# Experts of 144 to 192 slots: one gate-and-up product per pair of blocks, with the weights stationary, and empty slots left out of gathers and scatter-adds

## The chip, the cores and the metric

The kernel runs on one core of a Trainium2 chip. The metric is the device time of one execution in microseconds (us). The profile is one execution taken by the hardware profiler. Engines are named as there: PE is TensorE's matmul, PEld its weight load, DVE VectorE, ACT ScalarE, POOL GpSimd, SP SyncE, which issues the plain DMAs. A matmul's shapes are given as "stationary, moved": `128*128 128x512` holds 128 contracted rows by 128 columns in the array and moves 512 columns through it.

## What is computed

One block of a hybrid language model on 1024 tokens of width 1024: a mixer (two recurrent branches and an output projection), a layer norm, a mixture of experts, a layer norm. The change touches only the experts, which the reference computes like this:

```python
scores = sigmoid(h @ w_router)                 # 64 experts, 8 chosen for each token
for each expert e, on the tokens x that chose it, with their weights w:
    a = x @ w_gate[e]                          # 1024 -> 256
    u = x @ w_up[e]
    y = (silu(a) * u) @ w_down[e] * w          # 256 -> 1024
    acc[tokens] += y
out = layer_norm(alpha * h + acc + shared_expert(h))
```

## The kernel before

Everything is fp32. For precision each operand is split into a high part in a reduced fp32 format (`float32r`) and a low part, the remainder; a product is three matmuls, high x high, high x low and low x high (`mm3`, L135 to L137). The split of a weight piece of 128x1024 is a copy on ScalarE (L1529) and a subtraction on VectorE (L1530).

**Slots.** After the router, tokens are sorted on the chip into lists, one for each expert in the order of their counts. Each place in this order has a fixed cap (`CAPS`): 240, 208, three of 192, six of 176, nine of 160, eleven of 144, and 33 of 128, 112 or 96 slots. A place with more than 128 slots has two blocks, the first of 128 slots (m = 0), the second of the rest (m = 1). There are 64 + 31 = 95 blocks. Slots that no token fills point at rows behind the last token (index 1024 and up) of the gathered array `h1` and of the sum `acc`, which is 256 rows longer than the tokens for this purpose. Places with two blocks and places with one alternate in the order of work (`seq`), nearly throughout.

**A block's steps** (class `Block`): `fetch` gathers its rows of `h1` into an `xg` tile by an indirect DMA from GpSimd's queue, four blocks ahead; `turn_x` transposes them, 8 transposes of 128 columns into two PSUM tiles "tr" (there are two such banks), each of which ScalarE copies out as the high part (L173) and VectorE as the low part (L174); `gate_up` multiplies, with x stationary and the weights moved 512 columns at a time (256 of gate, 256 of up); `act` applies silu and the token's weight; `turn_a` transposes the result (L1431) and splits it; `down` multiplies by the down weights; `put` adds the rows to `acc` by an indirect DMA. A block of at most 64 slots is "packed": the high and low parts of x lie side by side as one stationary operand, so that two matmuls for each k do instead of three (`mm_packed`, L142 to L145), and the two halves of the result are added afterwards.

**The loop.** Iteration t works on block t and finishes block t-1. The instructions of PE, POOL and SP run in exactly the order of the code (`manual_schedule`); those of ScalarE and VectorE are ordered by a scheduler at build time. For PE an iteration is: the transposes of x of block t+1; half of gate and up of block t (k = 0 to 3); the matmuls that make a token list, if one is due (L1513); the transposes of the activation of block t-1; the other half of gate and up of t; down of t-1.

**Weights.** An expert's weights are six pieces of 128x1024, four of gate and up (two k each) and two of down. Raw pieces are loaded by SP ahead of time into nine tiles. The split halves live in eleven places that are used in turn, so a piece takes the place of the one eleven before it: piece 3 of an expert that of down piece 4 of the expert two before, and is split when that one's last reader is done. `splits` sends out splits at some 3 to 4.6 pieces an iteration, and always so many that the next block's gate and up have their four.

Of the kernel before, what the change touches and what calls it, by code (L numbers as in the profile page):

```python
# [19 lines left out]
P = 128  # L20
# [51 lines left out]
def block_kernel(tc, A, out):  # L72
# [1298 lines left out]
    between = mq.tile([P, 1], F32, name="between")  # L1371

    class Block:


        turn = 0

        def __init__(self, n, idx, wc, before=None):
            self.n, self.idx, self.wc, self.before = n, idx, wc, before

        def fetch(self):
            n = self.n
            self.x = mx.tile([P, D], F32, name="xg", tag="xg", bufs=XG)[:n]
            nc.gpsimd.indirect_dma_start(out=self.x, out_offset=None, in_=h1[:, :],  # L1384
                                         in_offset=bass.IndirectOffsetOnAxis(ap=self.idx, axis=0))

        def turn_x(self):

            n = self.n
            self.packed = n <= 64  # L1390
            if self.packed:
                xx = mt.tile([P, KT, P], F32R, name="xh", tag="xh", bufs=2)
                if n < 64:
                    nc.gpsimd.memset(xx[:, :, n:64].bitcast(F32), 0.0)
                self.xx, self.xh, self.xl = xx, xx[:, :, :n], xx[:, :, 64:64 + n]
            else:
                self.xh = mt.tile([P, KT, P], F32R, name="xh", tag="xh", bufs=2)[:, :, :n]
                self.xl = mt.tile([P, KT, P], F32R, name="xl", tag="xl", bufs=2)[:, :, :n]
# [16 lines left out]

        def act(self):
            n, pg = self.n, self.pg
            if self.packed:
                t = mo.tile([64, 512], F32, name="pk", tag="pk", bufs=2)[:n]
                nc.scalar.activation(t, pg[64:64 + n], AF.Copy)  # L1420
                nc.vector.tensor_add(t, pg[:n], t)
                pg = t
            self.a = ac = mo.tile([P, 256], F32, name="ac", tag="ac", bufs=2)[:n]
# [3 lines left out]
        def turn_a(self):  # L1427
            n = self.n
            pt = psum.tile([P, 4, P], F32, name="mm", tag="mm", bufs=3)
            for f in range(2):  # L1430
                nc.tensor.transpose(pt[:, f, :n], self.a[:, f * P:(f + 1) * P], ident[:n, :n])  # L1431
            if self.packed:
# [6 lines left out]
            nc.scalar.activation(self.ah, pt[:, 0:2, :n], AF.Copy)  # L1439
            nc.vector.tensor_sub(self.al, pt[:, 0:2, :n], self.ah.bitcast(F32))  # L1440

        def down(self):
# [3 lines left out]
            for half in range(2):  # L1446
# [3 lines left out]
                for f in range(2):  # L1450
# [3 lines left out]
                    else:  # L1454
                        mm3(py[:n], self.ah[:, f], self.al[:, f], wh, wl, f == 0, f == 1)
                if self.packed:
                    nc.scalar.activation(yh, py[64:64 + n], AF.Copy)
                    nc.vector.tensor_add(yh, py[:n], yh)
                else:
                    nc.scalar.activation(yh, py[:n], AF.Copy)  # L1460

        def put(self, apart=True):
            self.out = nc.gpsimd.indirect_dma_start(out=acc[:, :],  # L1463
                                                    out_offset=bass.IndirectOffsetOnAxis(ap=self.idx, axis=0),
                                                    in_=self.y, in_offset=None, compute_op=OP.add)
            if self.before is not None and apart:
                tc.declare_no_dep(self.out.ins, self.before.out.ins, reason="other tokens of the same expert")

    def finish_lists(pl, n, m, which=0):
# [8 lines left out]
        nc.vector.tensor_add(wc[:, :, 0], wc[:, :, 0], ls[:, :, 5])  # L1478
        return idx, wc

# [22 lines left out]
    def list_sums(q):  # L1503
# [12 lines left out]
        for m in range(nb):  # L1516
            n = min(P, cap - m * P)
            idx, wc = finish_lists(pl[:n, m], n, LG, m)
            for j in range(LG):
                x = seq[1 + q - LG + j]  # L1520
                nq = min(n, CAPS[x] - m * P)
                if nq > 0:
                    blocks[x, m] = Block(nq, idx[:nq, j], wc[:nq, j], before=blocks[x, 0] if m else None)

# [38 lines left out]
    with man:  # L1563
# [10 lines left out]
        for t in range(N + 1):  # L1574
# [43 lines left out]
    with tc.tile_pool(name="ov", bufs=1) as ov:  # L1618
# [41 lines left out]
        nc.vector.tensor_copy(tabr, pt[:, 0:2])  # L1660
        eidb = ov.tile([1, P], I32, name="eidb")
        nc.vector.tensor_copy(eidb, pt[0:1, 2])
# [3 lines left out]
        with tc.For_i(0, n_blocks, 1) as b:  # L1666
# [22 lines left out]
            for i in range(NT):  # L1689
                nc.tensor.matmul(pl[:, 0], oh[:, i], ab[:, i], start=i == 0, stop=i == NT - 1)  # L1690
            idx, wc = finish_lists(pl, P, 1)
            blk = Block(P, idx[:, 0], wc[:, 0])
            blk.fetch()
            blk.turn_x()
# [188 lines left out]
```

## Time and profile before

| | us |
|---|---|
| median of 3 runs | 2366.02 |
| lowest, highest | 2357.46, 2366.94 |
| the profiled execution, its own time | 2359.28 |
| its span, first to last instruction | 2357.4 |
| PE busy in the span | 2270.2 |
| DVE, ACT, POOL busy | 1570.2, 1102.0, 392.0 |
| bytes moved by DMA | 477.01 MB |

The span lies 1.9 us below the execution's own time. Busy is time with at least one instruction in flight; matmuls are pipelined, so a busy PE is not a PE at its peak, and the distance between the starts of two matmuls is the price of one rather than its duration. The experts take the stretch from about 1447 to 2312 us.

### The profile page before, as it was taken

How to read it: one execution, taken by the hardware profiler on the slowest of the kernel's cores; microseconds unless marked ns; L12 is line 12 of the kernel's file. 1: busy time of each engine (PE TensorE's matmuls, PEld its weight loads, DVE VectorE, ACT ScalarE, POOL GpSimd, SP SyncE). 2: the span in 40 equal slices, each digit the busy share in tenths (PEclk: the TensorE clock that was granted, in tenths of full speed). 3: DMA queues.
4: the chain of work that ended last, by engine and by line, in shares of the span. 5: the costliest groups of instructions: out<-in, count | busy, mean ns of one | idle time of the engine just before them, and what ended most of it. 6: DMA issues, size and time to landing. Idle time of an engine off the chain costs nothing.

```text
span 2357.4 us, 40161 instructions
## 1 busy us (share of the span) xinstructions
PE 2270.2 (96%) x15177; PEld 1804.1 (77%) x15177; DVE 1570.2 (67%) x3041; ACT 1102.0 (47%) x1853; POOL 392.0 (17%) x286
## 2 busy tenths in 40 slices
PE   7999999999999999999999999999999999999992
PEld 5797779877879977787887877777777777777761
DVE  6523886288614656214586677888888888888884
ACT  3432223223213265222332324677677777777773
POOL 4200000000000000000000001243434444433331
PEclk9999999999999999999999999999999999999996
DMA  7233244234322354536463336999999999999986
GB/s 289 89 115 123 74 139 131 91 114 130 106 81 82 121 180 170 165 99 232 146 225 115 119 124 221 301 336 319 327 324 336 321 314 319 327 307 324 305 285 166
DMA packets 203507, 477.01 MB, mean 202 GB/s; under 512 B 18720, under 2 KB 67552, under 8 KB 203312
## 3 DMA queue, kind: packets, MB, share of 16 engines
q1 hardware_dynamic: 180752, 396.13, 48.1%
q0 software_dynamic: 21520, 75.51, 13.4%
q8 instruction: 120, 1.97, 0.3%
q10 hardware_dynamic: 1040, 2.79, 0.3%
q14 instruction: 75, 0.61, 0.1%
HBM read 372.16 MB, written 103.78 MB: 202 GB/s over the span
## 4 chain that ended last, share of the span: by engine, by line
PE 85%; DVE 7%; DMA 3%; ACT 2%; issue 2%; POOL 0%; SPq 0%; DVEq 0%; POOLq 0%; ACTq 0%
PE mm L135 20%; PE mm L136 19%; PE mm L137 19%; PE sc L137 3%; PE tr L171 3%; PE sc L136 3%; PE sc L135 3%; PE mm L143 2%; PE mm L145 2%; PE sc L753 1%; PE po L1513 1%; DMA a<-qT 1%; PE sc L143 1%; PE mm L1431 1%; DVE wl L197 1%
## 5 line engine op out<-in xcount | busy, mean ns | idle before, releaser
L197 DVE TENSOR_TENSOR wl<-wraw,wh 128x1024 fp32r<-128x1024 f32 x118 | 141.4, 1221 | 205.4 <-ACT wh L196 201.3
L136 PE MATMUL mm<-hL,wh 128*128 128x512 f32 (+2 forms) x768 | 278.2, 362 | 0.0
L137 PE MATMUL mm<-hH,wl 128*128 128x512 f32 (+2 forms) x768 | 277.6, 361 | 0.0
L135 PE MATMUL mm<-hH,wh 128*128 128x512 f32 (+2 forms) x768 | 277.2, 361 | 0.0
L1463 POOL DMA_INDIRECT acc<-yo,idx x95 | 184.4, 1941 | 514.8 <-ACT xh L173 124.6
L135 PE MATMUL mm<-wh,hH 128*128 128x512 f32 x512 | 208.6, 407 | 2.6 <-ACT hH L349 1.8
L136 PE MATMUL mm<-wl,hH 128*128 128x512 f32 x512 | 209.0, 408 | 1.3 <-DVE wl L287 1.3
L137 PE MATMUL mm<-wh,hL 128*128 128x512 f32 x512 | 206.3, 403 | 0.0
L135 PEld LDWEIGHTS mm<-hH,wh 128*128 128x128 f32 x768 | 144.4, 188 | 17.2 <-issue 0.8
L136 PEld LDWEIGHTS mm<-hL,wh 128*128 128x128 f32 x768 | 144.4, 188 | 16.3 <-issue 0.5
L137 PEld LDWEIGHTS mm<-hH,wl 128*128 128x128 f32 x768 | 144.6, 188 | 15.6 <-issue 0.2
L196 ACT ACTIVATE wh<-wraw 128x1024 fp32r<-128x1024 f32 x118 | 122.7, 1056 | 54.0 <-PE mm L136 36.8
L1530 DVE TENSOR_TENSOR wl<-eraw,wh 128x1024 fp32r<-128x1024 f32 x112 | 135.4, 1216 | 14.9 <-ACT wh L1529 14.7
L1384 POOL DMA_INDIRECT xg<-h,idx x95 | 136.9, 1441 | 48.1 <-issue 22.8
L1530 DVE TENSOR_TENSOR wl<-wraw,wh 128x1024 fp32r<-128x1024 f32 x96 | 115.8, 1216 | 29.0 <-ACT wh L1529 28.6
L1529 ACT ACTIVATE wh<-eraw 128x1024 fp32r<-128x1024 f32 x112 | 117.2, 1061 | 19.0 <-PE mm L137 13.8
L135 PE MATMUL mm<-wh,xh 128*128 128x512 f32 (+3 forms) x296 | 123.7, 418 | 0.0
L135 PEld LDWEIGHTS mm<-wh,hH 128*128 128x128 f32 x512 | 98.2, 192 | 25.3 <-ACT hH L349 2.4
L136 PE MATMUL mm<-wl,xh 128*128 128x512 f32 (+3 forms) x296 | 117.1, 396 | 0.0
L137 PE MATMUL mm<-wh,xl 128*128 128x512 f32 (+3 forms) x296 | 116.9, 395 | 0.0
L137 PEld LDWEIGHTS mm<-wh,hL 128*128 128x128 f32 x512 | 97.7, 191 | 22.9 <-DVE hL L350 0.8
L136 PEld LDWEIGHTS mm<-wl,hH 128*128 128x128 f32 x512 | 98.0, 191 | 21.6 <-DVE wl L287 1.6
(550 smaller groups left out, 5424.9 us busy)
## 6 DMA issues: line engine op xcount, KB each, us to landing
eraw<-in_wexp_dram SPq DMA_DIRECT2D x210, 512.0 KB, 7.9
wraw<-in_wexp_dram SPq DMA_DIRECT2D x168, 512.0 KB, 6.9
wraw<-in_w_in_dram SPq DMA_DIRECT2D x72, 512.0 KB, 4.6
sgT<-st SPq DMA_DIRECT2D x32, 256.0 KB, 3.3
sg<-sgT SPq DMA_DIRECT2D x32, 256.0 KB, 4.2
wraw<-in_w_branch_a_dram SPq DMA_DIRECT2D x16, 512.0 KB, 5.0
wraw<-in_w_branch_b_dram SPq DMA_DIRECT2D x16, 512.0 KB, 6.9
wraw<-in_w_out_dram SPq DMA_DIRECT2D x16, 512.0 KB, 5.2
```

Of the source, the lines that this page charges most:

```text
L135: nc.tensor.matmul(o, ah, bh, start=start, stop=False)
L136: nc.tensor.matmul(o, ah, bl, start=False, stop=False)
L137: nc.tensor.matmul(o, al, bh, start=False, stop=stop)
L143: nc.tensor.matmul(o[:n], a[:, :n], bl, start=False, stop=False)
L145: nc.tensor.matmul(o[:w + n], a[:, :w + n], bh, start=False, stop=stop)
L171: nc.tensor.transpose(pt[:, k, :n], src[:, c:c + P], ident[:n, :n])
L196: nc.scalar.activation(h, raw, AF.Copy)
L197: (nc.gpsimd if j in on_pool else nc.vector).tensor_sub(l, raw, h.bitcast(F32))
L1384: nc.gpsimd.indirect_dma_start(out=self.x, out_offset=None, in_=h1[:, :], in_offset=bass.IndirectOffsetOnAxis(ap=self.idx, axis=0))
L1463: self.out = nc.gpsimd.indirect_dma_start(out=acc[:, :], out_offset=bass.IndirectOffsetOnAxis(ap=self.idx, axis=0), in_=self.y, in_offset= ...
L1529: nc.scalar.activation(h, raw, AF.Copy)
L1530: (nc.gpsimd if j in POOL_SPLITS else nc.vector).tensor_sub(l, raw, h.bitcast(F32))
```

## The change

For the 29 places of 144 to 192 slots the two blocks become a joined pair. The first block (`second` set) carries the matmuls of gate and up for both: `turn_x` transposes the x of both into one tile of up to 192 columns, and `gate_up` takes the weights as the stationary operand, in four column groups of 128 (two of gate, two of up), and moves the 144 to 192 columns of x through, for all eight k in each group. Its result comes out transposed, in two PSUM tiles, so that `turn_a` is not needed; `act` makes the activation for both blocks at once, and the tokens' weights are applied when `down`'s result is copied out. In the iteration of the second block (`joined`) `turn_x`, `gate_up`, `act` and `turn_a` do nothing. `down` and `put` of both blocks come together, in the iteration after it. `down` itself is unchanged (mm3 for the first block, packed for the second).

Slots without a token: both indirect DMAs get a bound of the last token, above which an index is skipped. As the rows skipped in a gather would otherwise be undefined, the five `xg` tiles become fixed ones that are cleared once. Places of 240 and 208 slots and those of one block work as before.

```diff
+    xgs = [mx.tile([P, D], F32, name="xg", tag="xg", bufs=XG) for _ in range(XG)]
+    for t in xgs:
+        nc.gpsimd.memset(t, 0.0)
...
+            self.joined = before is not None and n <= 64
+            if self.joined:
+                before.second = self
...
             nc.gpsimd.indirect_dma_start(out=self.x, out_offset=None, in_=h1[:, :],
-                                         in_offset=bass.IndirectOffsetOnAxis(ap=self.idx, axis=0))
+                                         in_offset=bass.IndirectOffsetOnAxis(ap=self.idx, axis=0),
+                                         bounds_check=T - 1, oob_is_err=False)
...
         def turn_x(self):
...
+            if self.joined:
+                return
+            if self.second is not None:
+                w = n + self.second.n
+                self.xh, self.xl = (mt.tile([P, KT, 192], F32R, name=q, tag=q, bufs=2)[:, :, :w] for q in ("xh", "xl"))
+                for b, c in ((self, slice(0, n)), (self.second, slice(n, w))):
+                    transpose_split(self.xh[:, :, c], self.xl[:, :, c], b.x, b.n)
+                return
...
         def gate_up(self, w, ks):
...
+            if self.second is not None:
+                n += self.second.n
+                if 0 in ks:
+                    self.w = w
+                    self.pg, self.pu = (psum.tile([P, 512], F32, name="mm", tag="mm", bufs=3)[:, :2 * n]
+                                        .rearrange("p (f n) -> p f n", f=2) for _ in range(2))
+                hs, ls = self.w()
+
+                for f in (0, 1) if 0 in ks else (2, 3):
+                    for k in range(KT):
+                        c = slice((k % 2) * 512 + f * P, (k % 2) * 512 + f * P + P)
+                        mm3((self.pg, self.pu)[f // 2][:, f % 2], hs[k // 2][:, c], ls[k // 2][:, c],
+                            self.xh[:, k], self.xl[:, k], k == 0, k == KT - 1)
+                return
...
         def act(self):
+            if self.joined:
+                return
             n, pg = self.n, self.pg
+            if self.second is not None:
+                w = n + self.second.n
+                a = mo.tile([P, 384], F32, name="ac", tag="ac", bufs=2)[:, :2 * w].rearrange("p (f n) -> p f n", f=2)
+                nc.scalar.activation(a, pg, AF.Silu)
+                nc.vector.tensor_mul(a, self.pu, a)
+                self.halves_a(a[:, :, :n])
+                self.second.halves_a(a[:, :, n:w])
+                return
...
         def turn_a(self):
+            if self.joined or self.second is not None:
+                return
...
         def down(self):
...
-                if self.packed:
+                if self.joined:
+                    nc.scalar.activation(yh, py[64:64 + n], AF.Copy, scale=self.wcp)
+                    nc.vector.scalar_tensor_tensor(yh, py[:n], self.wc, yh, op0=OP.mult, op1=OP.add)
+                elif self.packed:
...
+                elif self.second is not None:
+                    nc.scalar.activation(yh, py[:n], AF.Copy, scale=self.wc)
...
         def put(self, apart=True):
...
-                                                    in_=self.y, in_offset=None, compute_op=OP.add)
+                                                    in_=self.y, in_offset=None, compute_op=OP.add,
+                                                    bounds_check=T - 1, oob_is_err=False)
...
-            if prev:
-                prev.down()
+
+            for b in [] if not prev or prev.second is not None else [prev.before, prev] if prev.joined else [prev]:
+                b.down()
                 if t + AHEAD >= N:
                     nc.gpsimd.memset(between, 0.0)
-                prev.put()
+                b.put()
```

`halves_a` is the second part of `turn_a` (copy and subtraction into `ah` and `al`, or into the packed tile), now a function. `wcp` is a copy of the second block's token weights in partitions 64 and up.

## Rows read from the trace of the kernel before

**Rows 1.** Stage table, 1447 to 2312 us: length, busy and count by engine, clock, DMA.

```profile
core 0: us, PE busy (x) PEld busy (x) DVE busy (x) ACT busy (x) POOL busy (x), PEclk, DMA share, GB/s
1447.00:2312.00 865.00, 861.50 (x5002) 644.36 (x5000) 721.36 (x1110) 629.66 (x979) 322.12 (x213) 1.00 0.97 312
```

**Rows 2.** Waits of PE, 1460 to 2290 us: total, times, longest.

```profile
PE sc L137 <- DVE al L1440: 3.2, 10, 0.3
```

**Rows 3.** Timeline of PE, a 160-slot expert: start, length, engine, line, operation, tiles.

```profile
1820.44 0.68 PE L171 MATMUL tr<-ident,xg 32*128 32x32 f32 x8
1821.05 0.50 PE L135 MATMUL mm<-mh,xh 128*128 128x512 f32 x1
...
1823.96 0.64 PE L1513 MATMUL po<-aux,oh 128*128 128x6 bf16 x16
1824.53 0.44 PE L1431 MATMUL mm<-ident,ac 128*128 128x128 f32 x2
1824.72 0.48 PE L135 MATMUL mm<-ml,xh 128*128 128x512 f32 x1
...
1827.59 0.39 PE L135 MATMUL sc<-eh,ah 128*128 128x512 f32 x1
...
1830.37 1.03 PE L171 MATMUL tr<-ident,xg 128*128 128x128 f32 x8
1831.16 0.48 PE L142 MATMUL mm<-mh,xh 128*96 128x512 f32 x1
...
1833.10 0.64 PE L1513 MATMUL po<-aux,oh 128*128 128x6 bf16 x16
...
1833.86 0.47 PE L143 MATMUL mm<-ml,xh 128*32 128x512 f32 x1
...
1835.79 0.40 PE L135 MATMUL sc<-wh,ah 128*128 128x512 f32 x1
```

**Rows 4.** Timeline of PE, the router's first matmuls.

```profile
1211.72 0.22 PE L1105 MATMUL po<-wr,mh 128*128 128x128 f32 x1
1211.78 0.27 PE L1106 MATMUL po<-wr,ml 128*128 128x128 f32 x1
1211.89 0.28 PE L1105 MATMUL po<-wr,mh 128*128 128x128 f32 x1
```

**Rows 5.** Timeline of PE, a projection that moves 346 columns.

```profile
82.56 0.32 PE L536 MATMUL mm<-hH,gw 128*128 128x346 f32 x1
82.72 0.32 PE L537 MATMUL mm<-hL,gw 128*128 128x346 f32 x1
```

**Rows 6.** Timeline of ACT and DVE behind the transposes of 1830.37.

```profile
1831.31 1.08 ACT L173 ACTIVATE xh<-tr 128x512 fp32r<-128x512 f32 x2
1832.11 1.28 DVE L174 TENSOR_TENSOR xl<-tr,xh 128x512 fp32r<-128x512 f32 x2
```

**Rows 7.** Timelines of DVE and PE where a second block's down ends.

```profile
1823.41 1.20 DVE L1530 TENSOR_TENSOR wl<-wraw,wh 128x1024 fp32r<-128x1024 f32 x1
...
2233.92 0.67 PE L171 MATMUL tr<-ident,xg 16*128 16x16 f32 x8
2235.30 1.20 DVE L1530 TENSOR_TENSOR ml<-wraw,ml 128x1024 fp32r<-128x1024 f32 x1
```

**Rows 8.** Stage table of PE near the start: length, PE busy, clock, DMA.

```profile
42.00:46.00 4.00, 4.00 (x23) 1.00 0.66 224
46.00:49.00 3.00, 1.23 (x6) 0.98 0.78 248
49.00:52.00 3.00, 3.00 (x8) 0.50 0.37 149
```

**Rows 9.** DMA issues, 1447 to 2312 us: count, median us to landing.

```profile
xg<-h,idx POOLq DMA_INDIRECT x90, 9.6
```

**Rows 10.** Groups by line of POOL, 1447 to 2312 us: busy, mean ns.

```profile
L1394 POOL MEMSET xh<- 128x384 f32 x11 | 5.3, 483 | 0.0
```

**Rows 11.** Timeline of POOL, the first gather, with the idle time before it.

```profile
1434.61 1.89 POOL L1384 DMA_INDIRECT xg<-h,idx  x1 [11.13 <-DVE wc L1477]
```

More of the change, by code (lines that the diff above doesn't have):

```diff
@@ L1371, in block_kernel, with __init__ @@
     between = mq.tile([P, 1], F32, name="between")
+    xgs = [mx.tile([P, D], F32, name="xg", tag="xg", bufs=XG) for _ in range(XG)]
+    for t in xgs:
+        nc.gpsimd.memset(t, 0.0)
     class Block:
         turn = 0
-        def __init__(self, n, idx, wc, before=None):
+        fetched = 0
+        def __init__(self, n, idx, wc, before=None, wcp=None):
             self.n, self.idx, self.wc, self.before = n, idx, wc, before
+            self.second, self.wcp = None, wcp
+            self.joined = before is not None and n <= 64
+            if self.joined:
+                before.second = self
         def fetch(self):
             n = self.n
-            self.x = mx.tile([P, D], F32, name="xg", tag="xg", bufs=XG)[:n]
+            self.x = xgs[Block.fetched % XG][:n]
+            Block.fetched += 1
             nc.gpsimd.indirect_dma_start(out=self.x, out_offset=None, in_=h1[:, :],
-                                         in_offset=bass.IndirectOffsetOnAxis(ap=self.idx, axis=0))
+                                         in_offset=bass.IndirectOffsetOnAxis(ap=self.idx, axis=0),
+                                         bounds_check=T - 1, oob_is_err=False)
         def turn_x(self):
@@ L1431, in turn_a, with halves_a @@
                 nc.tensor.transpose(pt[:, f, :n], self.a[:, f * P:(f + 1) * P], ident[:n, :n])
+            self.halves_a(pt[:, 0:2, :n])
+        def halves_a(self, a):
+            n = self.n
             if self.packed:
@@ L1438, in turn_a @@
                 self.al = mo.tile([P, 2, P], F32R, name="al", tag="al", bufs=2)[:, :, :n]
-            nc.scalar.activation(self.ah, pt[:, 0:2, :n], AF.Copy)
-            nc.vector.tensor_sub(self.al, pt[:, 0:2, :n], self.ah.bitcast(F32))
+            nc.scalar.activation(self.ah, a, AF.Copy)
+            nc.vector.tensor_sub(self.al, a, self.ah.bitcast(F32))
         def down(self):
@@ L1455, in down @@
                         mm3(py[:n], self.ah[:, f], self.al[:, f], wh, wl, f == 0, f == 1)
-                if self.packed:
+                if self.joined:
+                    nc.scalar.activation(yh, py[64:64 + n], AF.Copy, scale=self.wcp)
+                    nc.vector.scalar_tensor_tensor(yh, py[:n], self.wc, yh, op0=OP.mult, op1=OP.add)
+                elif self.packed:
                     nc.scalar.activation(yh, py[64:64 + n], AF.Copy)
                     nc.vector.tensor_add(yh, py[:n], yh)
+                elif self.second is not None:
+                    nc.scalar.activation(yh, py[:n], AF.Copy, scale=self.wc)
                 else:
@@ L1478, in finish_lists @@
         nc.vector.tensor_add(wc[:, :, 0], wc[:, :, 0], ls[:, :, 5])
-        return idx, wc
+        wcp = None
+        if which:
+            wcp = mq.tile([P, 8, 1], F32, name="wcp", tag="wcp", bufs=3)
+            nc.vector.tensor_copy(wcp[64:64 + min(n, 64), :m], wc[:min(n, 64)])
+        return idx, wc, wcp
     order = []
@@ L1522, in list_sums @@
                 if nq > 0:
-                    blocks[x, m] = Block(nq, idx[:nq, j], wc[:nq, j], before=blocks[x, 0] if m else None)
+                    blocks[x, m] = Block(nq, idx[:nq, j], wc[:nq, j], before=blocks[x, 0] if m else None,
+                                         wcp=wcp[64:64 + nq, j] if m and nq <= 64 else None)
     def split_piece(q):
@@ L1690, in block_kernel @@
                 nc.tensor.matmul(pl[:, 0], oh[:, i], ab[:, i], start=i == 0, stop=i == NT - 1)
-            idx, wc = finish_lists(pl, P, 1)
+            idx, wc, _ = finish_lists(pl, P, 1)
             blk = Block(P, idx[:, 0], wc[:, 0])
+            xgs[Block.fetched % XG] = mx.tile([P, D], F32, name="xg", tag="xg", bufs=XG)
+            nc.gpsimd.memset(xgs[Block.fetched % XG], 0.0)
             blk.fetch()
```

14 lines of the change are left out of this document (8 added, 6 removed).

## The prediction

> **What bounds the kernel now.** I read the stage table first. From 1447 to 2312 us the kernel works through the experts, and there TensorE has something in flight for 861.5 of 865 us at a granted clock of 1.00 (2.4 GHz), while VectorE is busy 721, ScalarE 630, GpSimd 322 and the DMA engines are at 0.97 [rows 1]. Two resources are thus near full; the waits of TensorE decide between them. In 830 us it waited 3.2 us, ten times, for a VectorE result, and never for a weight or a gathered row [rows 2]. So this stage lasts as long as TensorE's own instruction stream, which is issued in the order of the code. A microsecond put into that stream, or a wait put in front of its head, is a microsecond of the run; VectorE's 17% of slack and the DMA queues are cover. The timeline of TensorE then gives the price of each piece of one expert of 160 slots [rows 3].
>
> **The change, part by part.** 29 of the 64 experts have 144 to 192 slots, and become "joined" pairs (a first block of 128, a second of 16 to 64). The two larger ones keep the old way.
>
> *Gate and up.* Before, 24 matmuls of 512 columns for the first block and 16 for the second. Their halves take 2.91, 2.87, 1.94 and 1.93 us: 9.65 us, or 0.2325 per matmul and 0.1 for each restart [rows 3]. After, the weights are stationary: 4 column groups x 8 k x 3 products = 96 matmuls, each of only 144 to 192 columns (mean 160.6), each with its own 128x128 weight load. The work in columns falls from 20480 to about 15400. The trace before has no such shape. The nearest row below is the router, the same kind of operands with 128 columns moved: its first two matmuls start 0.06 us apart, so 128 columns stream in that time, but the following ones start 0.11 apart [rows 4]. What fills the rest is the load of the next stationary operand, which can't start before the one ahead of it is in. The nearest row above is 346 columns: 0.16 us [rows 5]. 160 columns lie next to the router, and I take 0.111 for all sizes: 96 x 0.111 + 2 x 0.1 = 10.86 us, **1.21 us more** than before. Lower bound: no load shows, and the line through 346 columns at 0.159 and 512 at 0.2325 (0.44 ns a column) goes on, 0.077 each, 7.6 us, 2.05 less. Upper bound: the router's 0.111 was set by its columns and grows with them, 0.139 each, 13.5 us, 3.9 more.
>
> The Trainium skill ("TensorE: Matmul & The Clock Gate", section "LDWEIGHTS (loading the stationary operand)") has a load cost its columns at 1.2 GHz, 107 ns for 128, and its section on weight-path modes excludes fp32 from the fast load; by that, gate and up would take 96 x 107 ns = 10.2 us. This speaks against the change, and the router's 0.11 agrees.
>
> *The activation.* The two pairs of transposes of it go, 0.19 us a pair [rows 3]: 0.38 us off the stream. Gate and up come out transposed, so the product with the weight column moves to the scale of the last copy. ScalarE and VectorE lose a few small instructions a pair; they work beside TensorE [rows 1], so that counts as nothing. Net so far +0.83 us a pair.
>
> *Where the transposes of x stand.* Before, each block's 8 transposes (two "tr" banks) were separated from the next block's by gate and up, and their banks had been emptied long ago. Now the iteration of a second block holds no matmul of its own: the stream after the single-block expert's down product is 8 transposes for the next single block, a list sum, 8 transposes for the next pair's first block, 8 for its second, and only then a gate and up. That is six "tr" fills in a row through two banks. The row gives a bank's way back: transposes begin at 1830.37, ScalarE's copies at 1831.31, VectorE's subtractions run from 1832.11 to 1833.39 [rows 3, 6]. The first bank is free 2.4 us after its start, the second at 3.0. So fills 3 and 4 start at 2.4 and 3.0, fills 5 and 6 at 4.8 and 5.6, and the last ends at 5.9 us; without waiting the six and the list sum would take 0.79 + 0.79 + 0.61 + 0.57 = 2.76 [rows 3]. **Stall 3.1 us a pair.** Bounds: with nothing else in either queue, ScalarE's 0.54 and VectorE's 0.64 us a fill [rows 6], the last fill ends at about 4.95, 2.2 lost; two weight splits of 1.2 us [rows 7] ahead of the pair's copies make it 5.5. Queued behind the stalled transposes is everything TensorE still has to do.
>
> *Piece 3 of the weights.* The fourth piece of a pair's gate and up goes into the room of a down piece of the pair before, so its split starts when that pair's second down product ends. Before, it was wanted last: in this row the split ended at 1823.41 + 1.20, 4.17 us after the down product (1820.44), and it was used in the last quarter of the pair's first product, from the middle of 1824.72 to 1827.59 on, 1826.2 [rows 3, 7]. Now the first column group runs through all eight k, directly behind that down product, and wants piece 3 after 18 x 0.111 = 2.0 us. With the quickest row, 2236.50 against 2233.92, it comes after 2.58 [rows 7]; with 4.17 the wait is 2.2. I take 1.0, nearer the quick one because no copies of x compete there any more; bounds 0 and 2.2.
>
> *The clock.* At 46 to 49 us TensorE was busy 1.23 of 3 us, and the next 3 us were granted 0.50 (1.2 GHz): 8 matmuls against 23 in the 4 us before [rows 8]. The new stretch of transposes is 5.9 us with gaps, about 6 x 0.6 us busy. That lies between the stretch that lost the clock and those that kept it, so I take half of one loss of 1.5 us (such a stretch of 3 us at half clock does half its work): 0.75, bounds 0 and 1.5.
>
> *Slots without a token.* The caps add up to 9024 slots and there are 1024 x 8 = 8192 tokens to place, so 832 rows are no longer fetched or added. The gathers land 9.6 us after issue [rows 9], four blocks ahead, and TensorE waits for none [rows 2]: 0. Were that cover gone, each late microsecond would be one of the run. A bounds check in GpSimd's descriptor work is not in the trace; GpSimd has more than half of the stage free [rows 1], so between nothing and a doubling it stays 0. The five cleared buffers cost at most 5 x 1.3 us of GpSimd (0.483 for 384 columns, by proportion), ahead of the first gather, before which GpSimd stood idle for 11.1 us [rows 10, 11]: 0, or 6 us once if their room is freed late.
>
> **Sum.** 29 x 0.83 = 24 us, and 28 x (3.1 + 1.0 + 0.75) = 136 us (the first joined pair has no such neighbours): 160 us. The profiled execution took 2359.3 us, so 2519; the median of the runs lies 6.7 above it, so **2526 us**. With all lower bounds of the waits 24 + 62 gives 2452, with all upper ones 24 + 258 gives 2648.
>
> **The rivals.** (A) *The loads hide.* Each matmul costs its columns, 0.077 us: 29 x (-2.05 - 0.38) = -70, and the waits of 136 remain: +66, 2432 us. For it: 346 and 512 columns hide theirs [rows 3, 5]. Against: the router. The skill's section "Back-to-back issue gap" on the same page gives columns at 2.4 GHz plus 2.5 ns, 69 ns for 160, which is this rival.
> (B) *The banks are no bound*: the copies out keep up and piece 3 is early, only +24 stays: 2390. Against it: 2.4 us for one bank in a trace in which nothing hurried, but also nothing pressed.
> (C) *Faster*: A and B at once. The stream is 2.43 us a pair shorter and no wait takes its place: -70, 2296. It decides as soon as loads hide and the three waits together stay under 2.5 us a pair; the lower bound of the bank wait alone is 2.2.
> (D) *Loads and columns add up* (0.139 each): 29 x (3.9 - 0.38) + 136 = +238, 2604.
> That the joining does nothing can't be: the instruction counts change.
>
> **How the numbers follow.** Forecast 0.57, A 0.12, B 0.12, C 0.12, D 0.07. The range from 2385 to 2640 takes in B at its lower end, A, D and nearly all of the forecast's own spread (2452 to 2648); it leaves out C and the end of the tail. Faster by over 0.5% (about what a measurement here can tell from no change) is C: 0.12. Within 0.5% lies only the ground between C and B: 0.03. Slower 0.85.
>
> **What would show it.** Weight-stationary matmuls 0.11 us apart, whatever their columns (0.08 says A, 0.14 D). Waits of TensorE's transposes for VectorE's "xl" in rows that were empty before, some 3 us a pair; a wait of the weight-stationary line for a split's low half, about 1 us a pair; stretches granted about half clock within the stage; no wait for gathers. The prediction is wrong if the transposes' waits are missing, which B and C need, or if the first matmuls behind the pair's down product run through.

## The result, and the profile after

The changed kernel takes 2605.73 us (median of 4 runs, 2599.14 to 2606.34); the kernel before, beside it, 2365.43 (4 runs). The ratio is 1.1024 with a 95% interval of 1.1004 to 1.1044: slower by 10%, where 2526 was forecast. The profiled execution took 2599.14 us against 2359.28, 239.9 more, and the stage of the experts holds all of it: it ends at about 2552 instead of 2312 us, 1105 us instead of 865.

The stage table of after, cut at 2480 us, ahead of the stage's last pairs, with the columns of [rows 1]; then PE's waits over the whole stage, as in [rows 2]:

```profile
1447.00:2480.00 1033.00, 914.59 (x6112) 766.94 (x6111) 672.06 (x1014) 600.75 (x865) 259.83 (x174) 0.90 0.80 245
```

```profile
PE tr L171 <- DVE xl L174: 122.8, 66, 3.3
```

PE was in flight in all but 3.5 us of this stage before; now it idles for 118 of 1033 us, its clock has fallen from 1.00 to 0.90, and VectorE, ScalarE and the DMA engines are less busy than before, so none of them has become fuller. One wait stands behind nearly all of the idle time, the transposes' for VectorE's "xl", which was not in the list before. No wait of PE for a gathered row or a weight has come in.

The timeline of PE through one pair's product, the down product of the single-block expert before it, the six fills of transposes, and the next gate and up:

```profile
1950.30 0.24 PE L135 MATMUL mm<-xh,ml 128*128 128x160 f32 x1
...
1951.71 0.28 PE L136 MATMUL mm<-xl,wh 128*128 128x160 f32 x1
1951.82 0.28 PE L137 MATMUL mm<-xh,wl 128*128 128x160 f32 x1
...
1952.50 0.27 PE L137 MATMUL mm<-xh,wl 128*128 128x160 f32 x1
...
1955.62 0.39 PE L1481 MATMUL mm<-ident,ac 128*128 128x128 f32 x2
1955.77 0.32 PE L135 MATMUL mm<-xh,ml 128*128 128x160 f32 x1
...
1961.18 0.43 PE L135 MATMUL sc<-mh,ah 128*128 128x512 f32 x1
...
1963.99 1.04 PE L171 MATMUL tr<-ident,xg 128*128 128x128 f32 x8
1964.87 0.63 PE L1578 MATMUL po<-aux,oh 128*128 128x6 bf16 x16
1968.30 1.25 PE L171 MATMUL tr<-ident,xg 128*128 128x128 f32 x8 [2.80 <-DVE xl L174]
1971.44 0.63 PE L171 MATMUL tr<-ident,xg 32*128 32x32 f32 x4 [1.89 <-DVE xl L174]
...
1972.60 0.80 PE L135 MATMUL mm<-wh,xh 128*128 128x512 f32 x1
...
1977.47 0.64 PE L1578 MATMUL po<-aux,oh 128*128 128x6 bf16 x16
```

Four readings, each a term of the sum. The 96 weight-stationary matmuls start 0.111 us apart and take 5.32 + 5.41 = 10.73 us (1950.30 to 1955.62, 1955.77 to 1961.18). The six fills and the list sum take from 1963.99 to 1972.60, 8.61 us, where 2.76 would do without waiting. The 12 matmuls of gate and up behind them take 4.87 us (1972.60 to 1977.47) instead of 2.87. And the first column group runs through without a gap, its first matmul with the low half of piece 3 starting at 1952.50, where piece 3 had been expected late.

The cycle shown is one of 25 in this trace in which six fills stand in a row. Over all of them the fills take 8.22 us on average (7.54 to 9.21) and the 12 matmuls behind them 4.86 (4.21 to 5.29), so the stall here lies a little above the mean and the matmuls at it. Not all of a stall is idle time: of the 5.85 us in this cycle 4.69 are, and the rest goes to transposes that run slower behind the waits.

The clock in the same place, a stage table of 3 us each:

```profile
1964.00:1967.00 3.00, 1.50 (x25) 1.37 (x23) 2.54 (x5) 2.61 (x6) 0.00 (x0) 1.00 0.16 63
1967.00:1970.00 3.00, 1.25 (x8) 0.84 (x8) 3.00 (x5) 2.80 (x5) 2.55 (x2) 1.00 0.42 122
1970.00:1973.00 3.00, 1.56 (x9) 1.40 (x10) 2.28 (x5) 0.74 (x3) 2.01 (x2) 0.52 1.02 168
1973.00:1976.00 3.00, 3.00 (x8) 2.32 (x8) 0.29 (x1) 0.38 (x1) 0.00 (x0) 0.50 0.98 330
```

PE was busy about half of the time from 1964 to 1970 us; then 0.50 was granted (1.2 GHz) for some 7 us, most of it during the next gate and up: 8 matmuls in 3 us.

What the banks waited for stands in the timelines of ScalarE and VectorE (the brackets give the idle time before, and what ended it):

```profile
1959.37 1.06 ACT L1595 ACTIVATE ml<-eraw 128x1024 fp32r<-128x1024 f32 x1 [2.83 <-PE mm L137]
1960.33 1.04 ACT L1595 ACTIVATE ml<-wraw 128x1024 fp32r<-128x1024 f32 x1
1961.28 1.99 ACT L1595 ACTIVATE wh<-wraw 128x1024 fp32r<-128x1024 f32 x2
...
1966.76 1.08 ACT L173 ACTIVATE xh<-tr 128x512 fp32r<-128x512 f32 x2
```

```profile
1951.31 1.23 DVE L1596 TENSOR_TENSOR wl<-wraw,wh 128x1024 fp32r<-128x1024 f32 x1 [0.34 <-DMA wraw<-in_wexp_dram]
...
1960.46 1.22 DVE L1596 TENSOR_TENSOR ml<-eraw,ml 128x1024 fp32r<-128x1024 f32 x1 [3.47 <-ACT ml L1595]
1961.61 1.22 DVE L1596 TENSOR_TENSOR ml<-wraw,ml 128x1024 fp32r<-128x1024 f32 x1
1962.74 1.22 DVE L1596 TENSOR_TENSOR wl<-wraw,wh 128x1024 fp32r<-128x1024 f32 x1
...
1964.28 1.22 DVE L1596 TENSOR_TENSOR wl<-wraw,wh 128x1024 fp32r<-128x1024 f32 x1
...
1966.42 1.22 DVE L1596 TENSOR_TENSOR mh<-eraw,mh 128x1024 fp32r<-128x1024 f32 x1 [0.46 <-ACT mh L1595]
1967.56 1.28 DVE L174 TENSOR_TENSOR xl<-tr,xh 128x512 fp32r<-128x512 f32 x2
```

The copies of x (L173, L174) come at the end of a row of weight splits. ScalarE stood idle for 2.83 us before the first of these, until the pair's last column group was past its first two k, which are the first piece. Every column group reads all four pieces, so all four rooms come free inside that last group, and the splits come one behind the other from there on: five of them stand ahead of the copies, with the pair's activation and the copies out of the down banks between them. Before, k was the outer order, and the rooms came free one after the other. The bank filled at 1963.99 is thus free at 1968.30, after 4.3 us where I had read 2.4 [rows 3, 6].

### The profile page after: what moved, and what is told of

Its sections match the earlier page's. It is cut to its first block, busy times and chain, and to the rows that moved or that the text cites. A ratio compares the mean times of both kernels' runs of the same rounds, so it can differ in the third digit from the quotient of the medians.

```text
span 2597.3 us, 43125 instructions
## 1 busy us (share of the span) xinstructions
PE 2387.2 (92%) x16685; PEld 1978.0 (76%) x16685; DVE 1558.3 (60%) x2999; ACT 1109.5 (43%) x1795; POOL 349.0 (13%) x266
## 5 line engine op out<-in xcount | busy, mean ns | idle before, releaser
L1522 POOL DMA_INDIRECT acc<-yo,idx x95 | 173.9, 1831 | 804.4 <-ACT yo L1519 369.5
L171 PE MATMUL tr<-ident,xg 128*128 128x128 f32 (+6 forms) x760 | 118.5, 301 | 124.5 <-DVE xl L174 122.8
L171 PEld LDWEIGHTS tr<-ident,xg 128*128 128x128 f32 (+6 forms) x760 | 95.5, 172 | 148.9 <-DVE xl L174 135.9
L196 ACT ACTIVATE wh<-wraw 128x1024 fp32r<-128x1024 f32 x118 | 122.7, 1056 | 54.4 <-PE mm L136 37.3
L137 PE MATMUL mm<-xh,wl 128*128 128x144 f32 (+3 forms) x472 | 129.9, 275 | 0.0
L135 PE MATMUL mm<-xh,wh 128*128 128x144 f32 (+3 forms) x472 | 129.9, 275 | 0.0
L136 PE MATMUL mm<-xl,wh 128*128 128x144 f32 (+3 forms) x472 | 129.7, 275 | 0.0
L1595 ACT ACTIVATE wh<-wraw 128x1024 fp32r<-128x1024 f32 x96 | 100.1, 1056 | 66.2 <-PE mm L137 39.5
```

Source lines behind the costliest of these rows:

```text
L135: nc.tensor.matmul(o, ah, bh, start=start, stop=False)
L136: nc.tensor.matmul(o, ah, bl, start=False, stop=False)
L137: nc.tensor.matmul(o, al, bh, start=False, stop=stop)
L171: nc.tensor.transpose(pt[:, k, :n], src[:, c:c + P], ident[:n, :n])
L196: nc.scalar.activation(h, raw, AF.Copy)
L1522: self.out = nc.gpsimd.indirect_dma_start(out=acc[:, :], out_offset=bass.IndirectOffsetOnAxis(ap=self.idx, axis=0), in_=self.y, in_offset= ...
```

## The experiments

The theory after the first look: 28 x (1.08 - 0.38 + 5.9 + 2.0) = 241 us, from a product paced by its weight loads, two banks that come back late, and the clock that goes with the gaps. That it meets the 240 us so closely is partly luck: it takes one cycle for 28, and the means over the 25 rows would give some 210 us; what the few pairs add whose fills stand otherwise was not read. The rivals: the skipped slots cost something, the copies' rate rather than the banks is the bound, the clock falls because of the product itself.

**No joining, slots still skipped.** The tiles that the joining widened have their old sizes again.

```diff
-            self.joined = before is not None and n <= 64
+            self.joined = False
```

> The changed kernel without the joining: every place of 144 to 192 slots works as two blocks as before, and only the empty slots are left out of gathers and scatter-adds, with the cleared buffers. My theory (the time is TensorE's instruction stream, which waits for no gather): the same as before, 2365 us, within 0.5%. Rival (the DMA engines, at 0.97 in this stage, are a second bound and the skipped rows count): faster, by up to the 9% of the rows' share, some 10 to 20 us.

Measured: 2360.13 us against 2363.84, ratio 0.9993 (0.9978 to 1.0009). Within this interval, 5 us at most, the bounds on gathers and scatter-adds and the cleared tiles neither cost nor bring anything; the 240 us are the joining's.

**The transposes spread.** x is transposed one working block ahead, two fills before gate and up, the pair's other two between its halves, so that no more than two stand in a row.

```diff
-            if t + 1 < N:
-                blocks[order[t + 1]].turn_x()
...
+            if ahead_:                      # the next block that has matmuls of its own
+                ahead_.turn_x((0,))
...
             if prev:
                 prev.turn_a()
+            if ahead_:
+                ahead_.turn_x((1,))
```

> The changed kernel with only the place of the transposes of x changed: they are sent out one working block ahead, two fills of the transpose banks before a gate and up, and for a pair the other two between its halves, so that no more than two fills stand in a row. Theory: the waits of the transposes for VectorE and the halved clock both come from the six fills in a row and vanish; what stays is the price of the 96 weight-stationary matmuls less the saved transposes, 29 x 0.7 = 20 us over before: about 2386 us, granted clock 1.00 in the stage. Rival (ScalarE and VectorE as such are too slow for the new work): waits of 3 us or more a pair remain and the time stays over 2480 us.

Measured: 2532.42 us, ratio 1.0731 (1.0698 to 1.0765). 73 us came back, not the 220 expected. The list of PE's waits from 1447 us on:

```profile
PE tr L171 <- DMA xg<-h,idx: 24.0, 11, 3.0
PE tr L171 <- DVE xl L174: 22.7, 29, 2.7
PE sc L142 <- ACT yo L1520: 22.0, 9, 5.3
```

The wait for the copies has nearly gone, as the theory has it, but two others were behind it. Gathers four blocks ahead are late when x is wanted a block sooner. And PE waits for ScalarE to empty a down bank; in ScalarE's timeline that copy is queued behind a weight split that itself waits for its raw piece:

```profile
1935.97 1.06 ACT L1598 ACTIVATE mh<-eraw 128x1024 fp32r<-128x1024 f32 x1 [2.73 <-DMA eraw<-in_wexp_dram]
1936.94 1.25 ACT L1520 ACTIVATE yo<-sc,wc 128x512 f32<-128x512 f32 x2
```

The mean clock of the span, 0.955, is still far from the 0.987 of before. A good part of that is another kind of loss than in after:

```profile
2219.00:2246.00 27.00, 27.00 (x118) 25.64 (x119) 9.46 (x13) 8.95 (x13) 2.27 (x2) 0.50 0.59 178
```

Four times in this run (from about 1604, 2069, 2219 and 2290 us) PE waits 2.4 to 3.0 us for a gathered row directly ahead of a pair's product, and the granted clock is then 0.50 for 24 to 27 us, through the whole product, with PE in flight nearly all of the time. The product takes some 21 us there instead of 10.7. So the late gathers cost far more than the 24 us that the list puts down to them.

**Fewer columns moved.** On `order`; only the first 64 columns of the two cross products are moved, the rest of them is left out.

```diff
-                        mm3((self.pg, self.pu)[f // 2][:, f % 2], hs[k // 2][:, c], ls[k // 2][:, c],
-                            self.xh[:, k], self.xl[:, k], k == 0, k == KT - 1)
...
+                        nc.tensor.matmul(o, wh, self.xh[:, k], start=k == 0, stop=False)
+                        nc.tensor.matmul(o[:, :64], wh, self.xl[:, k, :64], start=False, stop=False)
+                        nc.tensor.matmul(o[:, :64], wl, self.xh[:, k, :64], start=False, stop=k == KT - 1)
```

> As the run with the transposes moved, but the two cross products of gate and up (high by low and low by high) move only the first 64 of the 144 to 192 columns for the joined pairs; the rest of the cross products is left out. Theory (each weight-stationary matmul costs the load of its 128 columns, 0.111 us, whatever it moves): the same time as with all columns, within 0.5%. Rival (the columns moved set the price): 64 of 96 matmuls get at least 0.04 us cheaper, 29 x 64 x 0.04 = 74 us less.

Measured: 2631.4 us, one run, 99 more than `order`, where the same time was expected. PE's timeline in one product, at two moments, and the stage table around them:

```profile
1921.47 0.32 PE L1443 MATMUL mm<-xh,wh 128*128 128x160 f32 x1
1921.63 0.23 PE L1444 MATMUL mm<-xl,wh 128*128 128x64 f32 x1
1921.69 0.28 PE L1445 MATMUL mm<-xh,wl 128*128 128x64 f32 x1
1921.81 0.32 PE L1443 MATMUL mm<-xh,wh 128*128 128x160 f32 x1
...
1927.76 0.48 PE L1443 MATMUL mm<-xh,ml 128*128 128x160 f32 x1
...
1928.40 0.48 PE L1443 MATMUL mm<-xh,ml 128*128 128x160 f32 x1
```

```profile
1919.50:1923.00 3.50, 3.50 (x34) 3.50 (x32) 3.50 (x5) 2.82 (x4) 1.35 (x1) 1.00 1.01 365
1923.00:1926.50 3.50, 3.50 (x43) 3.45 (x42) 1.70 (x3) 0.82 (x2) 1.25 (x2) 0.93 1.05 269
1926.50:1930.00 3.50, 3.50 (x18) 3.50 (x18) 0.21 (x1) 0.00 (x0) 0.00 (x0) 0.50 0.98 315
```

At the full clock the triple takes 0.335 us, as with 160 columns in all three: the loads set the pace, not the columns, as the theory has it. The time missed because of the clock. In this product, with PE in flight in all of the 20 us before (1906 to 1926 us), the granted clock fell to 0.50, where the triple takes 0.64. The pace of the loads follows the clock.

**The activation after the transposes.**

```diff
-            if prev:
+            if prev and not late:
                 prev.act()
...
+            if late:
+                prev.act()
```

> The changed kernel with one line moved: in the iteration of a second block, the transposes of the next block's x and their copies are sent out ahead of the pair's activation, so that ScalarE and VectorE take them first where their order follows the code. Theory: the first bank's way back, 4.3 us in the changed kernel where 2.4 was counted, is long because the pair's activation and copies out of the down product stand ahead of it; with the order turned it comes back in about 2.5 us, and some 1.5 us a pair go: 2560 us or less. Rival (the weight splits in the same queues set it): no change, 2600 us.

Measured: 2602.67 us, one run. It tells nothing: ScalarE's and VectorE's order is the scheduler's, and in the trace the activation still stands ahead of the copies, as in after. How much of the 4.3 us the activation and the copies out of the down banks hold stays open.

**The loops of the product exchanged.** On after: k outside, the four column groups inside.

```diff
-                for f in (0, 1) if 0 in ks else (2, 3):
-                    for k in range(KT):
+                for k in ks:
+                    for f in range(4):
...
-                            self.xh[:, k], self.xl[:, k], k == 0, k == KT - 1)
+                            self.xh[:, k], self.xl[:, k], k == 0 and f % 2 == 0, k == KT - 1 and f % 2 == 1)
```

> The kernel after, with the loops of a pair's gate and up exchanged: each k runs through all four column groups, so the four pieces of the weights are done with one after the other, as in the kernel before; matmuls, loads and the six fills of transposes in a row stay. Theory: in the trace after, the first bank's way back is 4.3 us where I took 2.4, because all four pieces of a pair are in use until the last column group, so that four weight splits (ScalarE 1.0, VectorE 1.2 us each) start together at its end, directly ahead of the copies of x. With the rooms coming free one by one the way back falls to about 2.4 to 3 us, the stall from 5.9 to some 3.5, the clock loss from 2.0 to about 1: 28 x 3.4 = 95 us less than after, about 2510. Rival 1: six fills through two banks stall by themselves, whatever stands ahead of them: within 1% of 2606. Rival 2: the splits are late for their weights (DMA), and bunch anyway: the same.

Measured: 2549.74 us, ratio 1.0792 (1.0771 to 1.0812): 56 us less than after, a bit over half of what was expected. PE's timeline:

```profile
1943.56 1.03 PE L171 MATMUL tr<-ident,xg 128*128 128x128 f32 x8
...
1946.04 1.25 PE L171 MATMUL tr<-ident,xg 128*128 128x128 f32 x8 [0.98 <-DVE xl L174]
1949.18 1.23 PE L171 MATMUL tr<-ident,xg 32*128 32x32 f32 x8 [1.88 <-DVE xl L174]
1950.34 0.80 PE L135 MATMUL mm<-wh,xh 128*128 128x512 f32 x1
```

The first bank's way back is 2.48 us, the 2.4 of the prediction; the six fills end after 6.78 us instead of 8.61. 28 x 1.83 = 51 of the 56 us; the means over the 25 rows differ by the same 1.83 (6.39 against 8.22). The second round still takes 3.1 us, and the gate and up behind the fills is hardly quicker: its first 12 matmuls take 4.75 us on average, against 4.86 in after.

**PE kept busy in the waits.** On after: five matmuls that nobody reads ahead of each of the pair's four fills (`filler`), or seven ahead of the third and fifth only (`filler_gap`).

```diff
+            if fill and half == 0:                   # filler: if fill
+                wf = fill()[0][4]
+                pf = psum.tile([P, 512], F32, name="sc", tag="sc", bufs=2)
+                for k in range(7):                   # filler: 5
+                    nc.tensor.matmul(pf, wf[:, 0:P], wf[:, 0:512], start=k == 0, stop=k == 6)
```

> The kernel after, with five matmuls of 512 columns, read by nobody, put ahead of each of the pair's four fills of transposes (20 a pair, 4.65 us at full clock, where 5.9 us are waited). Theory: the 2.0 us a pair that the following gate and up loses (12 matmuls in 4.87 instead of 2.87 us) is the clock, lost in the waits of the transposes; with TensorE kept busy there the granted clock stays at 1.00, the waits for the banks stay, and the time falls by about 28 x 2.0 = 56 us, to 2550. Rival: the clock falls for another reason (the weight-stationary product ahead of it): then the half-clock stretches stay, the added matmuls take 9.3 us instead of 4.65 in them, and the time is 2606 or up to 100 us more.

> As the run 'filler', but with the added matmuls only where TensorE really waits: seven ahead of the third and seven ahead of the fifth of the six fills (the waits of the trace after there are 2.80 and 1.89 us; seven take 1.63). In 'filler' the granted clock was back (24 matmuls behind the transposes in 5.57 us), but the added matmuls ahead of the fourth and sixth fill made the stretch itself longer by as much. Theory: clock loss and bank wait are two separate terms; with the stretch no longer than in after, the 2.0 us a pair of the clock come back: 2606 - 56 = 2550. Rival: the copies out are what the whole stage waits for, and what the clock gives back is waited for at the next transposes: 2590 to 2606.

Measured: 2599.93 us for `filler`, one run, and 2557.05 for `filler_gap`, ratio 1.0816 (1.0794 to 1.0838). In `filler` the 24 matmuls of the next gate and up took 5.57 us, but the fills with what was added took 9.71 us (8.61 in after): what the clock gave back went into the added work. In `filler_gap`, PE's timeline from the gate and up behind the fills on:

```profile
1958.83 0.50 PE L135 MATMUL mm<-wh,xh 128*128 128x512 f32 x1
...
1961.69 0.46 PE L1583 MATMUL po<-aux,oh 128*128 128x6 bf16 x9
```

12 matmuls from 1958.83 to 1961.69, 2.86 us; the transposes (from 1950.44) take 8.39, little less than in after. Over the 25 rows the 12 matmuls take 2.91 us on average instead of 4.86, and the fills with what was added 8.14 instead of 8.22. So the clock is a term by itself, lost in the waits: 48.7 us, or 1.74 a pair.

**The transposes spread, k outside, gathers a block earlier.** The edits of `order` and `k_first`, with one gather more in flight from the 17th block on.

```diff
-            if t + AHEAD < N:
-                blocks[order[t + AHEAD]].fetch()
+            for q in (t + AHEAD, t + AHEAD + 1) if t == 16 else (t + AHEAD + (t > 16),):
+                if q < N:
+                    blocks[order[q]].fetch()
```

> The run 'order' (transposes moved one working block ahead and spread, 2532 us) with two edits more: the loops of gate and up exchanged as in k_first, and from the 17th block on each gather one block earlier. Theory: what was left in 'order' were waits for gathered rows (24 us), for the copy out of the down product queued behind a weight split on ScalarE (22), for the transposes' copies (20) and the clock that went with them. The earlier gather takes the first away, the even release of the weight rooms most of the second and third: 2420 to 2460. Rival: the clock in 'order' is lost in the weight-stationary product itself; then the waits go and at most 60 us are gained, 2470 or more.

Measured: 2429.56 us, ratio 1.0274 (1.0254 to 1.0295), as the theory had it. PE waits 2.3 us for gathers and 9.4 for "xl"; the 21.2 us for ScalarE's copy out of a down bank stay, against the theory. Of the four long stretches at 0.50 in `order` one is left, behind the one wait for a gather. Which of the two edits brought how much was not separated.

**Four banks for the six fills.** On after (`banks`) and on `k_first` (`banks_k`): the two fills of a pair's first block go through the down product's banks.

```diff
-                    transpose_split(self.xh[:, :, c], self.xl[:, :, c], b.x, b.n)
+                    transpose_split(self.xh[:, :, c], self.xl[:, :, c], b.x, b.n, "sc" if b is self else "tr")
```

> The kernel after, where the two fills of a pair's first block go through the two banks of the down product ('sc', idle then) and only the other four through 'tr': four banks for the six fills in a row; nothing else is changed. Theory: the two banks are what the transposes wait for. By the trace of after the down banks are copied out at 1966.9 and the first 'tr' banks at 1968.2 to 1968.8, where the third fill waited until 1968.3 and the fifth until 1971.44: the third goes at once or within 1 us, the fifth some 3 us earlier: stall from 5.9 to about 2.5, with 0.5 to 1 us of clock 28 x 4 = 112 less than 2606, about 2495. Rival: the rate of the copies out on ScalarE and VectorE, between the weight splits, is the bound and the banks only show it: the wait moves to another place, 2590 to 2606.

> The kernel k_first (2550 us) with the same four banks. There the first 'tr' bank was copied out 2.5 us after its fill began, the second round was late by a weight split and the slot list on VectorE. Theory: with both the even release of the weights and four banks the six fills run nearly through (stall 4.0 to about 1) and the clock loss falls below 1 us: 2550 - 28 x 4.3 = 2430, what 'order_k' reached with the order changed instead. Rival: as for 'banks', 2530 to 2550.

Measured: 2509.05 us (ratio 1.0624, 1.0595 to 1.0654) and 2437.20 (1.0333, 1.0289 to 1.0376), 97 and 112 us less than the kernels that they start from. PE's waits in `banks_k`:

```profile
PE tr L171 <- DVE xl L174: 14.1, 26, 2.7
PE sc L142 <- ACT yo L1517: 10.2, 7, 4.2
PE sc L171 <- DVE yo L1512: 6.6, 6, 1.6
```

31 us, against 122.8 in after; the stage clock is 0.99. In `banks` 29.6 us of waits for "xl" are left, and 24.3 for ScalarE's copy out of a down bank are new. Two banks were the bound: with four, the same copies on the same two engines do.

**One load fewer in three.** On `order` with the earlier gathers: high and low parts of x side by side as one moving operand; the sums are added afterwards. `wide_k` interleaves the last two column groups over k.

```diff
+                        nc.tensor.matmul(pf, hs[k // 2][:, c], self.xx[:, k], start=k == 0, stop=False)
+                        nc.tensor.matmul(pf[:, :n], ls[k // 2][:, c], self.xh[:, k], start=False, stop=k == KT - 1)
...
+                    nc.scalar.activation(t, pf[:, n:], AF.Copy)
+                    nc.vector.tensor_add(t, pf[:, :n], t)
```

> The run 'order' with the earlier gathers, and with the high and low halves of x side by side as one moving operand: each high half of the weights is loaded once and 2 x 160 columns are moved past it, then the low half of the weights with 160: 64 matmuls a pair instead of 96; the four sums are added behind it on ScalarE and VectorE. Theory: the pair's matmuls are paced by their weight loads (0.111 us each, however few the columns); 320 columns cost about 0.147 (by the line through 346 and 512 columns of before), so the product takes 32 x (0.147 + 0.111) = 8.3 us instead of 10.8: 73 us less than the same order without it, some 2400 to 2440. Rival: the pitch of 0.111 is set by columns plus something; then 320 columns cost about 0.222 and nothing is gained, 2490 to 2530.

> The run 'wide', with the last two column groups interleaved over k, so that the four pieces of a pair's weights are done with one after the other over half the product, not all in its last quarter. In 'wide' the triple of products takes 0.258 us as expected (0.184 + 0.074), 2.3 us a pair less than in 'order_k', but the time is only 14 us below that of 'order_k', which frees the weights evenly. Theory: the even release is worth the missing 50 us (28 x 1.9, the size that k_first showed): 2365 to 2385, level with before or 1% above. Rival: what limits 'wide' is VectorE and ScalarE, which are busy 80% and 71% of the stage with the added sums, and the DMA engines at 0.94: within 0.5% of 2416.

Measured: 2415.90 us (1.0219, 1.0197 to 1.0240) and 2410.30 (1.0187, 1.0155 to 1.0220). PE's timeline in `wide`:

```profile
1947.03 0.23 PE L1443 MATMUL mm<-xh,wl 128*128 128x160 f32 x1
1947.10 0.34 PE L1442 MATMUL mm<-xh,wh 128*128 128x320 f32 x1
1947.29 0.23 PE L1443 MATMUL mm<-xh,wl 128*128 128x160 f32 x1
1947.36 0.35 PE L1442 MATMUL mm<-xh,wh 128*128 128x320 f32 x1
```

0.26 us for what took 0.335. The sum was foreseen to the hundredth, its parts were not: 0.19 and 0.07 us between the starts instead of 0.147 and 0.111. The time lies in the expected range, 2400 to 2440, but the 73 us less than the same order without this edit are not shown, since that order was not run; `order_k`, which has the loops exchanged instead, is 14 us slower. The stage table of `wide_k`:

```profile
1447.00:2310.00 863.00, 806.41 (x5306) 668.05 (x5305) 697.14 (x1155) 623.39 (x1010) 281.48 (x176) 0.96 0.92 296
```

PE idles for 57 of 863 us at a clock of 0.96; VectorE is at 81%, ScalarE at 72, the DMA engines at 0.92. PE's longest waits are 28.5 us for copies of x and 15.1 for a down bank. The even release that brought 56 us to after brings some 6 here, with intervals that overlap, so the theory of `wide_k` fell. Which of the three busy engines holds it wasn't separated. No version with the joining beat the kernel before.

## Why the prediction was right, and where its sizes were not

Slower was right, and so were the mechanisms of all terms but one: the wait for piece 3 never came. The size was short by 80 us. Per pair, predicted and measured in the cycle shown:

| step | predicted | measured | from |
|---|---|---|---|
| gate and up | +1.21 | +1.08 | 10.73 against 9.65 us |
| activation's transposes | -0.38 | -0.38 | gone from the stream |
| bank stall | 3.1 (2.2 to 5.5) | 5.9 | 8.61 - 2.76 us |
| piece 3 late | 1.0 (0 to 2.2) | 0 | no gap in the first column group |
| clock | 0.75 (0 to 1.5) | 2.0 in the timeline, 1.74 by `filler_gap` | 4.87 against 2.87 us |

The errors partly cancel: the stall is short by 2.8 us a pair and the clock by 1.0 to 1.25, while piece 3 gives back 1.0 that was never lost. Without that one the forecast would have been 28 us lower and further off.

*Gate and up, and rivals A and D.* 0.111 us a matmul whatever the columns, from 64 to 160: the router's row was the right neighbour, and `narrow` and `wide` show the load as the pace. In `narrow` PEld is in flight in all of 3.50 us with 32 loads, one behind the other at 0.11 us, as the prediction reasoned. Rivals A (0.08) and D (0.14) fall with it, and so does C, which needs A. The 2604 of D lies within 2 us of the measured time by chance: its 0.139 is in no row of after. The 69 ns by which the Trainium skill ("TensorE: Matmul & The Clock Gate", section "Back-to-back issue gap") spoke for A are its gap without the budget of a load; for a stream of loads and matmuls the same section has some 81 ns at 128 columns. The trace has 111 ns, and the measurement decides. The Trainium skill's section "LDWEIGHTS (loading the stationary operand)" on that page has 107 ns for 128 columns: at the full clock the trace agrees (0.111), at a granted 0.50 it does not (0.64 for three, 0.21 each), and again the measurement decides.

*The bank stall* is the step that failed in size. Its mechanism was the one predicted, and `banks` shows it by doubling the banks. But the way back of a bank was taken from a trace in which nothing stood ahead of the copies, and the upper bound from two weight splits ahead of them. There were five. The sentence on moving the weights past as the stationary operand counted matmuls and columns, and did not ask when a piece's last reader is now done; that was asked for piece 3 alone. `k_first` puts a size on it: 28 x 1.83 = 51 us in the fills, two thirds of the missing 2.8 us a pair. The rest lies in the second round, whose copies stand behind another split (1968.83) and the slot list (1969.97) on VectorE; no run took these away by themselves.

*Piece 3.* Its split began at 1951.31 and took 1.23 us; PE wanted the low half about 1952.5. Just in time, and no wait for a weight is in the list. The estimate from the quickest row of before, 0.6, was nearest, and the choice above it wrong. The prediction had named this as a sign against itself, the first matmuls behind the pair's down product running through, and they do: here not the size but the wait was wrong.

*The clock.* The mechanism, gaps between transposes, is shown by `filler_gap`. The loss was taken as half of one loss of 1.5 us, because the stretch seemed to lie between two known cases. It came in all of the 25 rows of six fills, and lasted longer than the stretch of [rows 8], 7 us instead of 3 in the cycle shown. Why it lasts longer is not shown: in `k_first` the fills are 1.83 us shorter, and the matmuls behind them lose about as much. One stretch was also a thin ground: in the profile of after PE is busy for 1.25 of the 3 us from 46 us on, much as in [rows 8], and the next 3 us are granted 1.00.

*Rival B*, the banks no bound, ended on 2390. The waits that it rules out are there. No run reached its time; `order_k` and `banks_k` come within 40 and 47 us of it, with edits that the change does not have.

*Slots without a token*: 0 predicted, 0.07% measured, within the interval.

## What to carry to other kernels

Before swapping which operand stands still, price the loads from a row of the same kernel, and ask for every buffer when its last reader is done in the new loop order: here one loop order let four weight rooms come free at once, ahead of the copies that TensorE waited for. When a step loses the matmuls that stood between its fills, count the banks that the fills in a row go through, and take a bank's way back with the work that is queued ahead of the copies, not from a quiet stretch. Where TensorE is busy 99% of a stage, a row of waits can cost twice: its own length, and the half clock behind it (here some 50 of 240 us).

## What the runs showed of the hardware

TensorE's clock can fall without a gap: in `narrow` PE was in flight in all of the 20 us from 1906 to 1926 us, at a granted 1.00, and then 0.50 (1.2 GHz) was granted, in a product whose two cross matmuls moved 64 columns, while in the cycle of after shown above the same product with 160 columns in all three ran at 1.00 to its end. Why it fell there, no run separates. Nor does an uninterrupted product bring the clock back at once: in `order` PE was in flight in all of 27 us at 0.50, behind a wait of 2.6 us. And a weight load is no fixed time: three loads with their matmuls took 0.335 us at a granted 1.00 and 0.64 at 0.50.
